# Output gates computed with tokens on partitions and 512 moving columns, split into 16-bit halves and reloaded by transposing transfers

## The chip, the cores and the metric

The kernel runs on one core of one Trainium2 chip. Inside the core, TensorE (PE) multiplies a stationary 128x128 block, loaded by a weight load (PEld), with a moving block; VectorE (DVE), ScalarE (ACT) and GpSimd (POOL) work element by element; SyncE (SP) issues most transfers between the chip's memory (DRAM) and the on-chip memory (SBUF). Products land in PSUM, eight banks of 128 partitions x 512 float32. The metric is device time in microseconds (us), the median of three runs. Transfers run on 16 DMA engines, in the order in which one queue issued them.

## The reference, cut to what matters

One layer of a diffusion backbone over T = 384 tokens (128 context, 256 latent), width D = 2048. The change touches the two sigmoid gates that merge the branches of the mixing sub-layer:

```python
gates = jax.nn.sigmoid(h @ lw['w_gate'] + lw['b_gate'])
g_a, g_b = jnp.split(gates, 2, axis=-1)
merged = g_a * (o @ lw['w_br_gla']) + g_b * (f @ lw['w_br_four'])
return merged @ lw['w_out'], s_f, s_b
```

`h` is 384 x 2048, `w_gate` 2048 x 4096. `o` comes from a gated linear attention (GLA), `f` from a Fourier branch. Everything is float32.

## The kernel before

**Products.** A float32 factor is held as two float32r parts, `hi` and `lo`, and each product is three matmuls: hi·hi, hi·lo, lo·hi. The normalised input is `hT` (tiles `A_hi`, `A_lo`), channels on partitions, 16 blocks of 128 channels by 384 tokens.

**Weight stream.** Weights come as tiles of 128 x 1024 float32 (512 KB) in the order of the list `srcs`. `load` issues one transfer into one of two `raw` buffers (L195); `split` casts it on ACT to `whi` (L223) and subtracts on DVE to get `wlo` (L224). There are four `whi` and four `wlo` buffers. `grab()` takes the oldest finished tile and, in the same breath, issues the next load and the next split. Three finished tiles stand ready while one is being multiplied, so the tile cast while tile k is multiplied is tile k+3, and its load was issued one tile earlier still, into the buffer that tile k+1 left when its `wlo` was made.

**Gate stage (L838 to L846).** For each of 32 blocks of 128 gate channels, `proj` takes two weight tiles and makes 48 matmuls into one PSUM bank of the pool `psm` (three banks, tag `mm`): stationary is a 128x128 block of weights, moving are the 384 tokens of `hT`. ACT adds the bias while it evicts to `gz` (L841), SP stores `gz` to DRAM `gates_d` (L842). After each weight tile `step(sd)` advances two side jobs by one step: `gla()`, the attention, which is cut into 61 steps by its `yield`s, and `ada`, which streams modulation weights (`adaw`, L569) into multiply-adds on DVE (L574).

**Mix stage (L1053 to L1080).** `mix_order` lists units: eight `o` (projection of the attention's output gate), sixteen `b` (`four`: Fourier products, stored to `four_d`), sixteen `a` (GLA product, multiplied by its gate, added to the Fourier part `yb`, written as `A_hi`/`A_lo` for the next projection). From the first `a` on the order is mostly b, a, a. Each `b` and `a` takes one gate: `gate_of` issues the load of a gate block (L968), for an `a` also of `yb` (L972), and takes the sigmoid of the oldest loaded one on ACT (L977). Weight tiles of `b` units are first folded on DVE (`ws`, L204 and L205).

**What sets the order.** In this part PE, ACT, DVE and POOL run strictly in the order in which the program was written; SP's order is made by a scheduler from estimated times. Every engine and every queue works in order, so an instruction that waits holds up all behind it.

Of the kernel before, what the change touches and what calls it, by code (L numbers as in the profile page):

```python
# [11 lines left out]
F32 = mybir.dt.float32  # L12
F32R = mybir.dt.float32r
U32 = mybir.dt.uint32
U16 = mybir.dt.uint16
# [6 lines left out]
P = 128  # L22
D = 2048
KT = D // P
TC = 128
TL = 256
T = TC + TL
# [70 lines left out]
def tile_step(ctx: ExitStack, tc: tile.TileContext, a, o):  # L98
# [44 lines left out]
    def two(w, i):  # L143
        return [w[i, 0], w[i, 1]]
# [4 lines left out]
    for i in range(32):  # L149
        srcs += two(a["w_gate"], i)  # L150
# [39 lines left out]
    def load(raw=None):  # L190
        n, src = next(srcs, (0, None))
        if src is not None:
            if raw is None:
                raw = wp.tile([P, G], F32, tag="raw", name="raw", bufs=2)
            SP.dma_start(raw, src)  # L195
            raws.append((raw, n in folded))
# [407 lines left out]
    gates_d = dram.tile([32, P, T], F32, name="gates_d")  # L604
# [9 lines left out]
    with ExitStack() as s:  # L614
# [23 lines left out]
        def gla():  # L638
# [10 lines left out]
            for h in range(NH):  # L649
# [12 lines left out]
                yield  # L662
# [90 lines left out]
                yield  # L753
# [32 lines left out]
                for t in range(3):  # L786
# [9 lines left out]
                    yield  # L796
# [41 lines left out]
        for i in range(32):  # L838
            def gate(p, i=i):
                g = pg.tile([P, T], F32, tag="gz", name="gz", bufs=2)  # L840
                ACT.activation(g, p, AF.Identity, bias=bgate[:, i : i + 1])  # L841
                SP.dma_start(gates_d[i], g)  # L842

            proj(psm, hT, gate, sd)
# [4 lines left out]
    four_d = dram.tile([KT, P, T], F32, name="four_d")  # L849
    with ExitStack() as s:  # L850
# [111 lines left out]
        def gate_of():  # L962

            u = next(gorder, None)
            if u is not None:
                b, i = u
                g = pc.tile([P, T], F32, tag="gate", name="gate", bufs=4)
                SP.dma_start(g, gates_d[i + (16 if b == "b" else 0)])  # L968
                y = None
                if b == "a":  # L970
                    y = pc.tile([P, T], F32, tag="yb", name="yb", bufs=4)
                    SP.dma_start(y, four_d[i])  # L972
                gates[u] = g, y
                raw_gates.append(g)
            if raw_gates and (u is None or len(raw_gates) > 1):
                g = raw_gates.pop(0)
                ACT.activation(g, g, AF.Sigmoid)  # L977
# [39 lines left out]
        for b, i in mix_order:  # L1017
            if b == "o":
                if i == 1:
                    gate_of()  # L1020
# [1002 lines left out]
```

## Time and profile before

| | us |
|---|---|
| median of 3 runs (1936.19 to 1936.66) | 1936.42 |
| the profiled execution | 1936.08 |
| its span, first to last instruction | 1934.3 |
| PE busy in the span | 1918.5 |
| matmuls of the gate stage, first to last eviction | 205.6 to 500.9 |
| mix stage, b and a units in turn | 680 to 740 |

The profile page gives busy time and counts per engine; the chain of waits follows the last instruction back to what released it; the window view gives each engine's busy time in a stretch of the span; the timeline and the tables by tile or line give single instructions and their mean durations. Where a row ends in "idle before, releaser", that is how long the engine stood still and what ended it. A matmul's own duration in the records contains its pipeline; what a run of them costs is read from the length of the run.

### The profile page before, as it was taken

Reading aid. Unit: us, or ns where it says so; the run is one execution under the profiler, and the core shown is the slowest. Engines: PE = TensorE matmul, PEld = TensorE weight load, DVE = VectorE, ACT = ScalarE, POOL = GpSimd, SP = SyncE. Lnnn points to the kernel's source line nnn. Section 1 sums busy time; section 2 is a strip of 40 time slices with the busy share of each in tenths; the row PEclk is TensorE's granted clock in tenths of the full one; section 3 lists DMA queues with packets and bytes.
Section 4 is the critical chain, followed back from the end, with each engine's and each line's share of the span. In section 5 each row is a group of like instructions: output and inputs, shape, how many; then the busy total and the mean of one; then the engine's idle time right before and its main releaser. Section 6 shows DMA issues by size and latency. Waiting matters only on the chain.

```text
span 1934.3 us, 27954 instructions
## 1 busy us (share of the span) xinstructions
PE 1918.5 (99%) x10398; PEld 1702.5 (88%) x10398; DVE 1641.8 (85%) x2059; ACT 1069.3 (55%) x1523; POOL 145.2 (8%) x171
## 2 busy tenths in 40 slices
PE   8999999999999999999999999999999999999998
PEld 5779999999999999999988888888888888888886
DVE  5569888879776797977789999999999999988885
ACT  4233454554335655446556666766666666666555
POOL 0000000000000000002100111111111120211001
PEclk9999999999999999999999999999999999999999
DMA  9978676767754687654639696979788797969553
GB/s 389 371 263 269 228 257 219 241 219 259 256 190 145 204 287 246 218 185 154 231 98 280 155 284 151 262 170 244 191 243 207 212 230 192 252 136 253 158 199 128
DMA packets 246152, 429.12 MB, mean 222 GB/s; under 512 B 45308, under 2 KB 149948, under 8 KB 241664
## 3 DMA queue, kind: packets, MB, share of 16 engines
q1 hardware_dynamic: 199072, 386.70, 60.0%
q0 software_dynamic: 18432, 33.56, 11.3%
q10 hardware_dynamic: 28512, 7.08, 2.3%
q8 instruction: 81, 1.33, 0.3%
q14 instruction: 55, 0.45, 0.1%
HBM read 365.68 MB, written 54.53 MB: 217 GB/s over the span
## 4 chain that ended last, share of the span: by engine, by line
PE 97%; DMA 1%; DVE 1%; ACT 0%; issue 0%; SPq 0%; POOL 0%; DVEq 0%; POOLq 0%; ACTq 0%
PE pmm L257 36%; PE pgu L1539 31%; PE pdn L1539 10%; PE pds L1539 7%; PE pv L399 3%; PE pgm L382 1%; PE pf L998 1%; DMA slab<-in_w_ada 1%; PE px L417 1%; PE pmm L1253 1%; PE pf L999 1%; PE bk L1539 1%; PE po L647 1%; PE pr L582 0%; PE dl L647 0%; PE pp L881 0%
## 5 line engine op out<-in xcount | busy, mean ns | idle before, releaser
L257 PE MATMUL pmm<-A_hi,whi 128*128 128x384 f32 x1200 | 404.3, 337 | 0.0
L257 PE MATMUL pmm<-A_hi,wlo 128*128 128x384 f32 x1200 | 401.4, 334 | 0.0
L257 PE MATMUL pmm<-A_lo,whi 128*128 128x384 f32 x1200 | 401.3, 334 | 0.0
L1437 ACT CAST whi<-u 128x1024 fp32r<-128x1024 f32 x200 | 210.1, 1053 | 173.1 <-PE pds L1539 42.6
L223 ACT CAST whi<-raw 128x1024 fp32r<-128x1024 f32 x181 | 189.8, 1051 | 171.3 <-DMA raw<-in_w_gate 62.2
L1448 DVE TENSOR_TENSOR wlo<-u,whi 128x1024 fp32r<-128x1024 f32 x200 | 243.7, 1220 | 34.1 <-ACT whi L1437 32.5
L224 DVE TENSOR_TENSOR wlo<-raw,whi 128x1024 fp32r<-128x1024 f32 x179 | 217.9, 1220 | 52.5 <-ACT whi L223 49.7
L1539 PE MATMUL pgu<-whi,A_hi 128*128 128x512 f32 x640 | 249.9, 390 | 0.0
L1539 PE MATMUL pgu<-whi,A_lo 128*128 128x512 f32 x640 | 249.2, 389 | 0.0
L257 PEld LDWEIGHTS pmm<-A_hi,whi 128*128 128x128 f32 x1200 | 225.3, 188 | 2.9 <-issue 1.8
L257 PEld LDWEIGHTS pmm<-A_lo,whi 128*128 128x128 f32 x1200 | 225.4, 188 | 0.2
L257 PEld LDWEIGHTS pmm<-A_hi,wlo 128*128 128x128 f32 x1200 | 225.3, 188 | 0.0
L574 DVE SCALAR_TENSOR_TENSOR adacc<-adaw,cond,adacc 128x1024 f32<-128x1024 f32 x180 | 222.7, 1278 | 2.8 <-DMA adaw<-in_w_ada 2.5
L1437 ACT CAST whi<-raw 128x1024 fp32r<-128x1024 f32 x157 | 165.0, 1053 | 87.2 <-PE pgu L1539 27.9
L1448 DVE TENSOR_TENSOR wlo<-raw,whi 128x1024 fp32r<-128x1024 f32 x157 | 191.1, 1218 | 12.6 <-ACT whi L1437 12.2
L1539 PE MATMUL pgu<-wlo,A_hi 128*128 128x512 f32 x640 | 185.8, 389 | 0.0
L1539 PEld LDWEIGHTS pgu<-whi,A_hi 128*128 128x128 f32 x640 | 120.1, 188 | 25.9 <-issue 0.8
L1539 PEld LDWEIGHTS pgu<-wlo,A_hi 128*128 128x128 f32 x640 | 120.1, 188 | 25.1
L1539 PEld LDWEIGHTS pgu<-whi,A_lo 128*128 128x128 f32 x640 | 120.1, 188 | 24.7
L1539 PE MATMUL pgu<-whi,S 128*128 128x512 f32 x400 | 116.6, 389 | 0.0
L1672 POOL DMA_DIRECT2D sums_d<-spare x64 | 58.5, 950 | 625.3 <-ACT spare L1668 618.9
L1539 PE MATMUL pdn<-whi,hid_hi 128*128 128x512 f32 x264 | 102.8, 389 | 0.0
(410 smaller groups left out, 3302.3 us busy)
## 6 DMA issues: line engine op xcount, KB each, us to landing
adaw<-in_w_ada SPq DMA_DIRECT2D x96, 512.0 KB, 4.2
raw<-in_w_d SPq DMA_DIRECT2D x70, 512.0 KB, 5.2
slab<-in_w_ada SPq DMA_DIRECT2D x32, 1024.0 KB
raw<-in_w_gate SPq DMA_DIRECT2D x64, 512.0 KB, 4.5
raw<-in_w_g SPq DMA_DIRECT2D x48, 512.0 KB, 3.7
raw<-in_w_u SPq DMA_DIRECT2D x48, 512.0 KB, 5.2
raw<-in_w_in SPq DMA_DIRECT2D x44, 512.0 KB, 4.3
u<-in_w_u SPq DMA_DIRECT2D x40, 512.0 KB, 7.1
```

What stands on the lines that cost most here:

```text
L223: ACT.copy(hi, raw)
L224: sub = lambda: eng.tensor_sub(lo, raw, hi.bitcast(F32))
L257: PE.matmul(dst, w[wi][:, k * n + n0 : k * n + n0 + P], x[xi][:, k0 + k, :], start=first and k == 0 and j == 0, stop=last and k == kts - 1 ...
L382: PE.matmul(pgv[q : q + 32, :], spad[:, k, :], slab[k // (KT // 2)][:, k % (KT // 2), :], start=k < 4, stop=k >= KT - 4,)
L399: PE.matmul(pv[2 * t + g], hT[x_][:, kb, t * P : (t + 1) * P], w_[:, g * 512 : (g + 1) * 512], start=kb == 0 and j == 0, stop=kb == KT - 1 ...
L417: PE.matmul(px, w_[:, u * P : (u + 1) * P], hT[x_][:, kb, :], start=j == 0, stop=j == 2)
L574: DVE.scalar_tensor_tensor(acc[:, c, :], w, cond[:, k, c : c + 1], acc[:, c, :], op0=ALU.mult, op1=ALU.add,)
L647: PE.matmul(dst, w[wi], x[xi], start=first and j == 0, stop=last and j == 2)
L1437: ACT.copy(hi, src)
L1448: DVE.tensor_sub(lo, src, hi.bitcast(F32))
L1539: PE.matmul(dst, stat[x_][m], mov(w[w_], m), start=first and w_ == m == x_ == 0, stop=last and w_ == m == 1, skip_group_check=any(more),)
L1672: POOL.dma_start(sums_d[k], u, accum_op=ALU.add)
```

## The change

`w_gate` is read in 64 tiles that hold four blocks of 128 gate channels and two blocks of 128 input channels, so that each partition's row is four pieces of 1 KB. For each of eight groups `q` of 512 gate channels, three PSUM banks `pgt` (128 tokens x 512 channels each, all three banks of `psm`) are filled by eight weight tiles (`m`), 18 matmuls each: stationary is a block of `hT` (128 channels x 128 tokens), moving are 512 weight columns. At m = 7, after each token block's last matmul, ACT copies the bank to `gz`, copies that as 16-bit halves, sorted, to `gpl`, and SP stores `gpl` to one of eight DRAM tensors. In the mix stage each gate block is read back by a transposing transfer (channels on partitions again), ACT puts the halves together, and the bias is now added in the sigmoid. The attention's side job has twelve `yield`s fewer (49 steps) and is not advanced at m = 6 and 7, where only `ada` is. `yb` is loaded at another place, the gate buffers are counted anew.

```diff
-    for i in range(32):
-        srcs += two(a["w_gate"], i)
+    for q in range(8):
+        for m in range(8):
+            src = a["w_gate"][4 * q : 4 * q + 4, m // 4, :, 256 * (m % 4) : 256 * (m % 4) + 256]
+            srcs.append(src.rearrange("n p x -> p n x"))
...
-    gates_d = dram.tile([32, P, T], F32, name="gates_d")
+    gates_d = [dram.tile([T, 2 * 512], U16, name=f"gates_d{n}") for n in range(8)]
...
                     SP.dma_start(s0[d], a["s0"][d, h])
-                yield
...
                     DVE.tensor_add(v, v, am[hf(c)])
-                yield
...
-                    yield
+                    if t:
+                        yield
...
-        for i in range(32):
-            def gate(p, i=i):
-                g = pg.tile([P, T], F32, tag="gz", name="gz", bufs=2)
-                ACT.activation(g, p, AF.Identity, bias=bgate[:, i : i + 1])
-                SP.dma_start(gates_d[i], g)
-
-            proj(psm, hT, gate, sd)
+        for q in range(8):
+            pt = [psm.tile([P, 512], F32, tag="mm", name="pgt") for _ in range(3)]
+            for m in range(8):
+                w = [x.rearrange("p (n k c) -> p n k c", n=4, k=2) for x in grab()]
+                for t in range(3):
+                    ts = slice(t * P, (t + 1) * P)
+                    for k in range(2):
+                        for j, (wi, xi) in enumerate(((0, 0), (0, 1), (1, 0))):
+                            PE.matmul(
+                                pt[t], hT[xi][:, 2 * m + k, ts], w[wi][:, :, k, :],
+                                start=m == k == j == 0, stop=m == 7 and k == 1 and j == 2,
+                            )
+                    if m == 7:
+                        g = pg.tile([P, 512], F32, tag="gz", name="gz")
+                        ACT.copy(g, pt[t])
+                        pl = pg.tile([P, 2 * 512], U16, tag="gpl", name="gpl", bufs=2)
+                        ACT.copy(
+                            pl.rearrange("p (n h c) -> p n h c", n=4, h=2),
+                            g.bitcast(U16).rearrange("p (n c h) -> p n h c", n=4, h=2),
+                        )
+                        SP.dma_start(gates_d[q][ts, :], pl)
+                step(ada if m in (6,7,) else sd)
...
-        def gate_of():
+        def gate_load():
 
             u = next(gorder, None)
             if u is not None:
                 b, i = u
-                g = pc.tile([P, T], F32, tag="gate", name="gate", bufs=4)
-                SP.dma_start(g, gates_d[i + (16 if b == "b" else 0)])
...
+                n = i + (16 if b == "b" else 0)
+                pl = pc.tile([P, 2 * T], U16, tag="gpl", name="gpl", bufs=4)
+                SP.dma_start(
+                    pl.rearrange("p (h t) -> p h t", h=2), gates_d[n // 4][:, 256 * (n % 4) : 256 * (n % 4) + 256],
+                    transpose=True,
+                )
+                raw_gates.append((u, pl))
...
+        def gate_of():
+
+            if raw_gates:
+                u, pl = raw_gates.pop(0)
+                b, i = u
+                n = i + (16 if b == "b" else 0)
+                g = pc.tile([P, T], F32, tag="gate", name="gate", bufs=3)
+                y = ys.pop(u, None)
+                y_load()
+                ACT.copy(
+                    g.bitcast(U16).rearrange("p (x h) -> p h x", h=2), pl.rearrange("p (h x) -> p h x", h=2),
+                )
+                ACT.activation(g, g, AF.Sigmoid, bias=bgate[:, n : n + 1])
                 gates[u] = g, y
...
+            gate_load()
```

Three places show how the instructions stand. ACT's queue in the gate stage, before: the casts of weight tiles (`whi<-raw`) with an eviction (`gz`) after every second one.

```order
L223 CAST whi<-raw 128x1024
L841 ACTIVATE gz<-pmm,bgate 128x384
L223 CAST whi<-raw 128x1024 x2
L841 ACTIVATE gz<-pmm,bgate 128x384
L702 ACT_TABLE_LOAD
```

The same queue in the changed kernel at the end of a group q; `pgt` are the three banks.

```order
L225 CAST whi<-raw 128x1024 x2
L853 COPY gz<-pgt 128x512
L855 COPY gpl<-gz 128x1024
L853 COPY gz<-pgt 128x512
L855 COPY gpl<-gz 128x1024
L853 COPY gz<-pgt 128x512
L855 COPY gpl<-gz 128x1024
L225 CAST whi<-raw 128x1024 x2
```

The evictions have moved together: six copies stand between two casts, and all of them behind the cast that the last tile's `grab` wrote.

ACT's queue in the mix stage, one group b, a, a, before (`fd` evicts the Fourier product, `A_hi` is the merged result's first part).

```order
L1002 COPY fd<-pf 128x194 x2
L223 CAST whi<-ws 128x1024
L977 ACTIVATE gate<-gate 128x384
L223 CAST whi<-raw 128x1024
L283 CAST A_hi<-yb 128x384
L977 ACTIVATE gate<-gate 128x384
```

The same stretch in the changed kernel.

```order
L1039 COPY fd<-pf 128x194 x2
L225 CAST whi<-ws 128x1024
L1009 COPY gate<-gpl 128x2x384
L1012 ACTIVATE gate<-gate,bgate 128x384
L225 CAST whi<-raw 128x1024
L285 CAST A_hi<-yb 128x384
L1009 COPY gate<-gpl 128x2x384
L1012 ACTIVATE gate<-gate,bgate 128x384
```

Each sigmoid has a copy ahead of it, which waits for a transposing transfer; the next cast of a weight tile stands behind both.

SP's queue over one such group, before.

```order
L1012 DMA four_d<-y 128x384
L968 DMA gate<-gates_d 128x384
L195 DMA raw<-in_w_br_four 128x1024
L972 DMA yb<-four_d 128x384
L968 DMA gate<-gates_d 128x384
L195 DMA raw<-in_w_br_gla 128x1024
L968 DMA gate<-gates_d 128x384
L195 DMA raw<-in_w_br_gla 128x1024
L972 DMA yb<-four_d 128x384
```

The same group in the changed kernel.

```order
L1049 DMA four_d_4629<-y 128x384
L985 DMA_TRANSPOSE gpl<-gates_d_1372 128x2x384
L998 DMA yb<-four_d_4624 128x384
L197 DMA raw<-in_w_br_four 128x1024
L985 DMA_TRANSPOSE gpl<-gates_d_1367 128x2x384
L197 DMA raw<-in_w_br_gla 128x1024 x2
L998 DMA yb<-four_d_4625 128x384
L985 DMA_TRANSPOSE gpl<-gates_d_1367 128x2x384
```

Three transposing transfers stand where three plain gate loads stood, and both loads of GLA weights now follow one of them directly.

More of the change, by code (lines that the diff above doesn't have):

```diff
@@ L837, in tile_step @@
         rate[0] = 1.0
[L838 to L844 removed]
+        for q in range(8):
[20 more added lines that the diff above has]
+                step(ada if m in (6,7,) else sd)
         for _ in gl:
             pass
[L849 removed]
+    four_d = [dram.tile([P, T], F32, name=f"four_d{n}") for n in range(KT)]
     with ExitStack() as s:
@@ L1018, in tile_step @@
             if b == "o":
[L1019 to L1020 removed]
+                if i < 2:
+                    gate_load()
+                    if i == 0:
+                        gate_load()
                 proj(psm, hT, lambda p: gcol(p, i), sd)
```

16 lines of the change are left out of this document (7 added, 9 removed).

## The prediction

> **What bounds the kernel now.** I read the page first, then the chain of waits, then windows, then single queues. The page, busy time and chain by engine:
>
> ```profile
> span 1934.3 us, 27954 instructions
> PE 1918.5 (99%) x10398; PEld 1702.5 (88%) x10398; DVE 1641.8 (85%) x2059; ACT 1069.3 (55%) x1523; POOL 145.2 (8%) x171
> PE 97%; DMA 1%; DVE 1%; ACT 0%; issue 0%; SPq 0%; POOL 0%; DVEq 0%; POOLq 0%; ACTq 0%
> ```
>
> PE works through 99% of the span and is 97% of the chain. So the time falls only where PE does its matmuls in less time, and rises only where PE is made to wait. The windows (PE, PEld, DVE, ACT, POOL, clock, DMA share, GB/s) show the two stages that the change touches, and ten-microsecond pieces at the place where PE is not full:
>
> ```profile
> 201.00:505.00 304.00, 304.00 (x1974) 299.46 (x1973) 258.81 (x329) 146.76 (x248) 1.87 (x6) 1.00 0.72 236
> 680.00:740.00 60.00, 59.28 (x359) 58.67 (x358) 53.95 (x103) 33.69 (x61) 0.00 (x0) 1.00 0.86 279
> 680.00:690.00 10.00, 9.46 (x58) 9.17 (x57) 7.46 (x18) 4.45 (x10) 0.00 (x0) 1.00 0.88 293
> 690.00:700.00 10.00, 9.81 (x60) 9.49 (x59) 9.00 (x17) 5.11 (x11) 0.00 (x0) 1.00 0.86 268
> ```
>
> In the gate stage (first row) PE never stops; DVE has 45 us of 304 free, ACT half. In the mix stage PE loses 0.54 and 0.19 us where a and b units begin to alternate, and DVE is busy 54 of 60 us: those who feed PE are at their limit there.
>
> **Term 1, the matmuls.** Pieces of the chain in order of time (start, length, what) give what a matmul costs in a run: 384 moving columns under L257, 512 under L1539, whose form (activations stationary, a strided half of a weight tile moving) is the one that the gate stage gets.
>
> ```profile
> 737.83 116.53 PE pmm L257 x672
> 1058.69 23.12 PE pgu L1539 x102
> 281.87 8.32 PE pmm L257 x48
> 454.42 4.20 PE pmm L257 x24
> ```
>
> 116.53/672 = 173.4 ns and 23.12/102 = 226.7 ns. The columns are the same in number; 32 x 48 = 1536 matmuls become 8 x 8 x 18 = 1152. 1536 x 173.4 = 266.4 us, 1152 x 226.7 = 261.1 us: **-5.2 us**, all of it on PE, which sets the end. The difference of the two lengths says why: 128 more columns cost 53.3 ns, so 384 cost 159.9 and some 13.5 ns belong to each matmul whatever its width. The gain would be nothing at 266.4/1152 = 231 ns, so 4.5 ns a matmul decide it.
>
> The Trainium skill speaks against this term: "TensorE: Matmul & The Clock Gate", section "Wait — 56ns, not 53.3ns?", puts a warm matmul at its columns over 2.4 GHz plus about 2.5 ns. By that the 384 matmuls fewer would be worth an estimated 1.0 us. The rows above disagree (13.5 ns, at a granted clock of 1.00), and I go by them.
>
> **Term 2, the three banks in the gate stage.** Before, three banks rotated and an eviction had the time of two blocks, 16.6 us (2 x 8.32). Now each group fills all three, and the next group's first matmul into a bank waits for the copy out of it. What stands ahead of these copies on ACT is the cast of a weight tile. The rows for the old eviction, for that cast (cast of tile k+3 while PE has tile k), and for what ACT waited for in this stage (total, times, longest):
>
> ```profile
> L841 ACT ACTIVATE gz<-pmm,bgate 128x384 f32<-128x384 f32 x32 | 18.6, 581 | 43.4 <-PE pmm L257 40.7 <-issue 2.6
> 282.03 1.04 ACT L223 CAST whi<-raw 128x1024 fp32r<-128x1024 f32 x1
> 459.05 1.05 ACT L223 CAST whi<-raw 128x1024 fp32r<-128x1024 f32 x1
> ACT whi L223 <- DMA raw<-in_w_gate: 57.1, 27, 6.9
> ```
>
> The copies' durations, from the same shapes later in the program (a bank of 512 columns to SBUF; 16-bit halves sorted; halves put together; the sigmoid):
>
> ```profile
> L1668 ACT COPY dw<-pds 128x512 f32<-128x512 f32 x45 | 24.3, 581 | 0.0
> L1613 ACT COPY ep<-ep 128x1024 uint16<-128x1024 uint16 x18 | 18.7, 1041 | 0.0
> L1622 ACT COPY ep<-ep 128x1024 uint16<-128x1024 uint16 x18 | 24.4, 1356 | 0.0
> L977 ACT ACTIVATE gate<-gate 128x384 f32<-128x384 f32 x32 | 16.8, 523 | 0.1
> ```
>
> A weight tile is now 18 x 226.7 = 4.08 us, 1.36 us for each token block. Count from PE's start of the tile m = 7. If the cast ends at e, the third bank is out at e + 3 x 0.58 + 2 x 1.04 = e + 3.8 us; PE wants it at 4.08 + 2 x 1.36 = 6.8. So PE waits e - 3.0 us at a group's end, nothing below. In the trace e lies between 1.2 us (tile from 281.87, cast ended 283.07) and 5.7 (tile from 454.42, cast ended 460.10), because the cast waits for its raw tile (57.1 us in 27 waits), whose buffer DVE frees late where the attention loads it. Bounds for eight ends: 0 and 8 x 2.7 = 21.6 us. Half of the ends fall behind attention steps that leave DVE free, and at m = 6 and 7 no attention step adds work, so I take nothing for four ends and the middle, e = 3.45, 0.45 us each, for four: **+1.8 us**.
>
> The rest of this stage I cost at nothing, with its cover. ACT gains 24 x (0.58 + 1.04) - 18.6 = 20.3 us in a stage in which it is idle for 157. The second `gpl` buffer makes the third sort wait for the first store, and behind it the next cast; stores land in 3.7 us, and three finished tiles (12.2 us) cover that once per 33 us. Without the cover each end would cost up to 4 us. The Fourier constants (L857) queue on SP behind the last store, as now; the raw loads behind them have the same three tiles. The twelve attention steps fewer move the same work. The rows for store, gate reload and the program's own transposing transfers, each with its time to landing, and the loads in 4 KB rows (gate weights now) and in shorter pieces:
>
> ```profile
> L842 SPq DMA_DIRECT2D gates_d<-gz x32: 326/327/425, 206.2 to 501.7; - x32
> DMA to landing us min/median/max: 2.5/3.7/5.3
> L968 SPq DMA_DIRECT2D gate<-gates_d x32: 319/424/795, 522.6 to 747.9; - x32
> DMA to landing us min/median/max: 2.4/3.9/5.8
> L1616 ACTq DMA_TRANSPOSE ep<-ep x18: 1249/1376/2142, 1050.5 to 1787.8; - x18
> DMA to landing us min/median/max: 5.3/8.9/11.7
> q1 hardware_dynamic: 199072, 386.70, 60.0%
> q10 hardware_dynamic: 28512, 7.08, 2.3%
> raw<-in_w_gate SPq DMA_DIRECT2D x64, 512.0 KB, 4.5
> raw<-in_w_g SPq DMA_DIRECT2D x48, 512.0 KB, 3.7
> raw<-in_w_u SPq DMA_DIRECT2D x48, 512.0 KB, 5.2
> ```
>
> Tiles in pieces land in 3.7 to 5.2 us, on both sides of the present 4.5: no change taken.
>
> **Term 3, the mix stage.** ACT puts each gate's halves together: 768/1024 x 1.356 = 1.02 us, 32 times. It stands ahead of the next cast. What follows shows whether that reaches PE (waits of PE in 600 to 765; ACT, then DVE, in one group b, a, a; the group's period):
>
> ```profile
> PE pmm L257 <- DVE gate L1033: 0.5, 1, 0.5
> PE pf L999 <- DVE wlo L224: 0.2, 1, 0.2
> 699.93 1.05 ACT L223 CAST whi<-ws 128x1024 fp32r<-128x1024 f32 x1 [2.81 <-DVE ws L205]
> 700.88 0.52 ACT L977 ACTIVATE gate<-gate 128x384 f32<-128x384 f32 x1
> 701.31 1.04 ACT L223 CAST whi<-raw 128x1024 fp32r<-128x1024 f32 x1
> 695.89 1.22 DVE L224 TENSOR_TENSOR wlo<-raw,whi 128x1024 fp32r<-128x1024 f32 x1 [0.90 <-ACT whi L223]
> 702.82 1.22 DVE L224 TENSOR_TENSOR wlo<-raw,whi 128x1024 fp32r<-128x1024 f32 x1
> 716.33 8.36 PE pmm L257 x48
> 727.08 8.36 PE pmm L257 x48
> ```
>
> A group lasts 10.75 us (716.33 to 727.08). The cast at 701.31 would end at 703.4 instead of 702.35; DVE wants it at 702.82, so DVE is 0.55 us late, once per group. The group's other casts had waited for DVE (2.81 us) or a raw tile, and hide the copy. Six groups: 3.3 us, out of the 6.05 us that DVE is idle in the window. Only where PE already waits, in the first two groups, does it come through: 1.1 us. The transfers add to it. Per MB a transposing one held the engines (2.3/7.08)/(60.0/386.70) = 2.1 times as long as the others. The window's seventeen gate blocks are 3.3 MB of 16.7, 0.17 of its 0.86 share; at 2.1 times, the engines are at their limit (0.86 + 0.17 x 1.1 = 1.05), and the raw loads behind them land later, as SP is also held about 1.0 us (6/8 of 1.376) instead of 0.42 for each. Bounds: 0, and 6 x 1.02 = 6 us; I take 0.8 us beside the 1.1, since DVE's idle 6 us absorb most: **+1.9 us**.
>
> On this the Trainium skill ("Advanced Engine Details and Errata", section "X-Bar Transpose (TRN2)") says that transposing transfers are as fast as regular ones. The two queue rows disagree (2.1 times). By the page the 0.8 us would go and the sum would be 0.8 us less.
>
> **Sum.** Span 1934.3, profiled execution 1936.08: 1936.1 - 5.2 + 1.8 + 1.9 = 1934.6 us. The median stands 0.3 us above the profiled execution, so the forecast is **1934.9 us**.
>
> **Rivals.**
> - *Nothing is given back* (25%): copies and transfers lie in idle time. For it: ACT half idle, every gate loaded three units ahead. Against it: the two stretches in which PE waits already. 1936.1 - 5.2 + 0.3 = 1931.2 us.
> - *The banks hold PE at every group's end* (17%): slower than before. For it: 57.1 us of waits for raw tiles ahead of these copies, and no spare bank. At e = 4.6, between the middle and the longest, 8 x 1.6 = 12.8 instead of 1.8: 1945.9 us. It decides from e = 3.4 on, at every end (8 x 0.43 us, with 1.9 in the mix stage, uses up the 5.2). Against it: PE waits only 0.7 us in all, and e was 1.2 at the easy tiles.
> - *Transposing transfers land too late* (14%): a gate is loaded three units ahead, one group, 10.75 us. Below that landing time it is hidden; above, ACT waits in every group. At 11.7, the longest seen, 6 x 0.95 = 5.7 us on top of term 2 and the 1.1: 1936.1 - 5.2 + 1.8 + 1.1 + 5.7 + 0.3 = 1939.8 us. Against it: the plain reload lands in 3.9 here, and the 8.9 belongs to a stage with much larger loads.
> - *The spacing is not saved* (6%): the fixed part per matmul is smaller here than under L1539's rows. At 1.0 us saved, 1939.1 us.
>
> **How the numbers follow.** Forecast 38%, own range 1932.5 to 1937.5. A measurement tells about 0.2% (3.9 us) from no change: below 1932.5 is faster, above 1940.3 slower. Faster: the first rival's 25 and 5 from the forecast's lower edge, 0.30. Slower: 17 from the banks, 6 from late transfers that land beyond 11.7, 2 from the forecast's upper edge, 0.25. Same: 0.45. The range goes from 1930.5 (the first rival, with attention steps that break up the matmuls less often) to 1943, which holds the late transfers and the lower part of the bank rival; some 15% lie outside.
>
> **What would show it.** Runs of `pgt` matmuls at 226 to 228 ns each show term 1. PE waits for ACT `gz` of 1 to 4 us in sum show term 2; over 8 us, the bank rival. In the mix stage PE busy of 57 to 59 in the sixty microseconds of b and a units, with ACT not waiting for the transposing transfers, shows term 3; ACT waits for `gpl` show the third rival. It is wrong if PE waits for `wlo` in the gate stage, or if the matmuls there take 230 ns or more.

## The result, and the profile after

The changed kernel takes 1960.47 us, the median of four runs (1958.69 to 1963.19), against 1936.31 us for the kernel before on the same chip: a ratio of 1.0127, 95% interval 1.0112 to 1.0142. It is slower by 24 us, where 1.5 us faster was forecast. The profiled execution took 1959.22 us. Its page, busy time and chain by engine:

```profile
span 1957.4 us, 27180 instructions
PE 1925.7 (98%) x10014; PEld 1655.7 (85%) x10014; DVE 1642.1 (84%) x2059; ACT 1125.6 (58%) x1571; POOL 145.3 (7%) x171
PE 79%; DVE 7%; DMA 6%; ACT 5%; issue 2%; SPq 0%; POOL 0%; ACTq 0%; DVEq 0%; POOLq 0%
```

PE has 384 matmuls fewer and is nevertheless busy 7 us longer, and its share of the chain falls from 97% to 79%: the chain now runs through the making of weight tiles (ACT, DVE, DMA) as well. Where the time went shows when each kernel reaches the same place in the program. The numbers are starts and ends of the named PE instructions in the two traces, in us:

| stretch | before | after | difference |
|---|---|---|---|
| up to the first gate matmul | 196.7 | 197.1 | +0.4 |
| gate stage, first matmul to the last one's end | 304.0 | 319.9 | +15.9 |
| from there to the first `px` (Fourier branch) | 20.8 | 20.7 | -0.1 |
| first `px` to the first `pst` after the mix stage (called mix stretch below) | 371.6 | 377.7 | +6.1 |
| from there to the last matmul's end | 1035.0 | 1036.4 | +1.4 |

Two thirds of the loss lie in the gate stage. Its windows (time, then busy time of PE, PEld, DVE, ACT, POOL, then granted clock, which is TensorE's clock as a share of its full speed, DMA share, GB/s): the whole stage, then five-microsecond pieces around its two longest stops.

```profile
197.10:517.00 319.90, 307.94 (x1590) 251.57 (x1590) 258.26 (x325) 166.32 (x262) 1.87 (x6) 0.98 0.70 222
317.00:322.00 5.00, 2.38 (x11) 1.63 (x9) 0.00 (x0) 1.15 (x2) 0.00 (x0) 1.00 0.54 187
322.00:327.00 5.00, 4.31 (x14) 3.49 (x15) 3.20 (x10) 4.28 (x9) 0.00 (x0) 0.71 0.32 97
442.00:447.00 5.00, 1.52 (x7) 0.94 (x5) 1.47 (x4) 3.83 (x5) 0.00 (x0) 1.00 0.35 106
447.00:452.00 5.00, 4.48 (x14) 3.81 (x15) 5.00 (x6) 4.26 (x6) 0.00 (x0) 0.50 0.10 17
452.00:457.00 5.00, 5.00 (x23) 4.18 (x23) 4.61 (x7) 0.47 (x2) 0.00 (x0) 0.82 0.67 206
```

Before, PE did not stop in this stage; now it stands 12 us. Each long stop has a second price: the pieces behind it run at a granted clock of 0.71, 0.50 and 0.82, so PE is busy and does less. Taken as the missing share of the clock, that is 5 x (0.29 + 0.50 + 0.18) = 4.9 us. DVE does nothing at all from 317 to 322, and behind the second stop (447 to 452) the loads fall to 17 GB/s: the weight stream paused as well.

What waited in the stage (waiting engine and tile, what it waited for; us in total, times, longest): DVE and ACT, then PE.

```profile
DVE wlo L226 <- ACT whi L225: 41.3, 19, 8.8
ACT gpl L855 <- DMA gates_d<-gpl: 13.2, 7, 3.9
PE bT L693 <- ACT lah L285: 4.2, 2, 3.5
PE ptm L593 <- ACT adacc L589: 3.3, 1, 3.3
PE pgt L847 <- ACT gz L853: 1.9, 2, 1.2
```

DVE's wait for `whi` was 16.1 us before:

```profile
DVE wlo L224 <- ACT whi L223: 16.1, 18, 2.9
```

PE never waits for `whi` or `wlo` in this stage: no gate matmul stood for want of a weight tile. ACT stands 13.2 us before the third sort of a group until the group's first store has landed. PE's waits for the banks (`gz`) are 1.9 us, as forecast (1.8); its two long waits are for operands of the side jobs that ACT makes: `lah`, read by the attention's matmul into `bT`, and `adacc`, read by the modulation job's matmul into `ptm`. The timeline of ACT at a group's end (start, length, line, operation, in brackets the idle time before it and what ended it) shows what they have to do with the store:

```profile
435.00 1.05 ACT L855 COPY gpl<-gz 128x1024 uint16<-128x1024 uint16 x1
436.08 0.59 ACT L853 COPY gz<-pgt 128x512 f32<-128x512 f32 x1
439.18 1.05 ACT L855 COPY gpl<-gz 128x1024 uint16<-128x1024 uint16 x1 [2.51 <-DMA gates_d<-gpl]
440.13 1.04 ACT L225 CAST whi<-raw 128x1024 fp32r<-128x1024 f32 x1
441.08 0.86 ACT L676 ACTIVATE la<-z 128x512 f32<-128x512 f32 x2
...
446.12 0.83 ACT L285 CAST lah<-la 128x768 fp32r<-128x768 f32 x1 [1.14 <-DVE la L680]
```

The store was issued at 434.38. Behind the sort that waited for it stand the cast of the next weight tile and the attention's chain up to `lah`, which ends at 446.95. PE's last gate matmul in front of the attention's `bT` ran out at 443.5, and it stood 3.48 us until 447.00, though gate matmuls stood behind `bT` in its queue whose `wlo` DVE had finished by 442.44. The stop at 319 is the same with `adacc`; the third sort, what ACT does behind it, and the matmul that waits for that:

```profile
321.32 1.04 ACT L855 COPY gpl<-gz 128x1024 uint16<-128x1024 uint16 x1 [3.85 <-DMA gates_d<-gpl]
322.27 0.37 ACT L589 COPY adacc<-pr 128x256 f32<-128x256 f32 x1
322.69 0.44 PE L593 MATMUL ptm<-ident,adacc 128*128 128x128 f32 x2 [3.32 <-ACT adacc L589]
```

The mix stage loses in another way. PE's waits in it, then one turn of ACT, SP and DVE through a group b, a, a (PE's own group is 10.75 us long):

```profile
PE pf L1036 <- DVE wlo L226: 5.2, 5, 1.4
717.19 1.05 ACT L225 CAST whi<-ws 128x1024 fp32r<-128x1024 f32 x1 [3.12 <-DVE ws L207]
718.15 1.07 ACT L1009 COPY gate<-gpl 128x768 uint16<-128x768 uint16 x1
719.25 0.62 ACT L1012 ACTIVATE gate<-gate,bgate 128x384 f32<-128x384 f32 x1
719.77 1.03 ACT L225 CAST whi<-raw 128x1024 fp32r<-128x1024 f32 x1
720.70 0.51 ACT L285 CAST A_hi<-yb 128x384 fp32r<-128x384 f32 x1
721.12 1.07 ACT L1009 COPY gate<-gpl 128x768 uint16<-128x768 uint16 x1
722.21 1.21 SPq L985 DMA_TRANSPOSE gpl<-gates_d  x1
723.54 0.50 SPq L998 DMA_DIRECT2D yb<-four_d  x1
724.15 0.37 SPq L197 DMA_DIRECT2D raw<-in_w_br_four  x1
728.26 0.69 DVE L206 TENSOR_TENSOR ws<-raw 128x512 f32<-128x512 f32 x1 [1.71 <-DMA raw<-in_w_br_four]
729.59 1.05 ACT L225 CAST whi<-ws 128x1024 fp32r<-128x1024 f32 x1 [3.35 <-DVE ws L207]
```

Follow it down: cast, gate copy, sigmoid, cast, `A_hi`, the second gate copy; 0.02 us after that copy's end SP issues the next transposing reload, which had waited for it; behind it in SP's queue stand `yb` and the Fourier weights' load, whose tile lands at 728.2, is folded, and can be cast at 729.59. That is a closed loop of 729.59 - 717.19 = 12.4 us in which nothing waits for PE, and it is longer than PE's 10.75. It holds for the other groups too: from 690 to 765, 16 of 18 reloads start 0.03 us after the end of a gate copy, and the casts of folded tiles are 12.3 us apart on average (705.03 to 754.28). SP's wait for ACT ahead of the reloads, which the profile puts down to the instruction behind the copy, the sigmoid:

```profile
SPq L985 <- ACT gate L1012: 19.7, 11, 3.3
```

### The profile page after: what moved, and what is told of

Same layout as the page of the kernel before. It is cut to its first block, busy times and chain, and to the rows that moved or that the text cites. A ratio compares the mean times of both kernels' runs of the same rounds, so it can differ in the third digit from the quotient of the medians.

```text
span 1957.4 us, 27180 instructions
## 1 busy us (share of the span) xinstructions
PE 1925.7 (98%) x10014; PEld 1655.7 (85%) x10014; DVE 1642.1 (84%) x2059; ACT 1125.6 (58%) x1571; POOL 145.3 (7%) x171
## 4 chain that ended last, share of the span: by engine, by line
PE 79%; DVE 7%; DMA 6%; ACT 5%; issue 2%; SPq 0%; POOL 0%; ACTq 0%; DVEq 0%; POOLq 0%
PE pgu L1578 31%; PE pmm L259 16%; PE pdn L1578 10%; PE pds L1578 7%; PE pgt L847 6%; PE pv L401 3%; DVE adacc L576 2%; DMA raw<-in_w_gate 2%; DVE wlo L226 2%; ACT whi L225 2%; PE pgm L384 1%; DMA raw<-in_w_br_four 1%; DMA slab<-in_w_ada 1%; PE px L419 1%; DMA gates_d<-gpl 1%
## 5 line engine op out<-in xcount | busy, mean ns | idle before, releaser
L1476 ACT CAST whi<-u 128x1024 fp32r<-128x1024 f32 x200 | 210.2, 1053 | 168.3 <-PE pgu L1578 38.7
L259 PE MATMUL pmm<-A_hi,whi 128*128 128x384 f32 x688 | 231.4, 336 | 0.0
L259 PE MATMUL pmm<-A_lo,whi 128*128 128x384 f32 x688 | 230.1, 334 | 0.0
L259 PE MATMUL pmm<-A_hi,wlo 128*128 128x384 f32 x688 | 230.0, 334 | 0.0
L847 PE MATMUL pgt<-whi,A_hi 128*128 128x512 f32 x384 | 153.3, 399 | 2.1 <-ACT gz L853 1.9
L847 PE MATMUL pgt<-wlo,A_hi 128*128 128x512 f32 x384 | 151.2, 394 | 0.0
L847 PE MATMUL pgt<-whi,A_lo 128*128 128x512 f32 x384 | 151.1, 394 | 0.0
L259 PEld LDWEIGHTS pmm<-A_hi,whi 128*128 128x128 f32 x688 | 129.2, 188 | 1.1 <-issue 1.0
L259 PEld LDWEIGHTS pmm<-A_lo,whi 128*128 128x128 f32 x688 | 129.2, 188 | 0.5 <-DVE A_lo L286 0.2
L259 PEld LDWEIGHTS pmm<-A_hi,wlo 128*128 128x128 f32 x688 | 129.1, 188 | 0.0
```

The source lines that it names most:

```text
L259: PE.matmul(dst, w[wi][:, k * n + n0 : k * n + n0 + P], x[xi][:, k0 + k, :], start=first and k == 0 and j == 0, stop=last and k == kts - 1 ...
L847: PE.matmul(pt[t], hT[xi][:, 2 * m + k, ts], w[wi][:, :, k, :], start=m == k == j == 0, stop=m == 7 and k == 1 and j == 2,)
L1476: ACT.copy(hi, src)
```

## The experiments

Each time is the median of four runs (the last but one: ten). Ratios are against the kernel before, run beside it, with 95% intervals. Gate stage and mix stretch are measured as in the table above, in one profiled execution of each, and such an execution can lie off the median: 1953.4 us for the third sort buffer, 1961.2 for the halves on POOL, 1953.9 for the side bank (some 7 of its 8 us too many lie behind the mix stretch). In the eight runs that have the change's mix stage unaltered the mix stretch is 377.7 to 381.0 us, so differences of 3 us in it are not told from none.

| run | time, us | ratio | gate stage | PE idle in it | mix stretch |
|---|---|---|---|---|---|
| change | 1960.5 | 1.0112 to 1.0142 | 319.9 | 12.0 | 377.7 |
| third sort buffer | 1949.8 | 1.0056 to 1.0086 | 310.8 | 5.9 | 381.0 |
| six reload buffers | 1962.0 | 1.0115 to 1.0145 | 320.2 | 12.2 | 381.4 |
| steps as before | 1964.7 | 1.0134 to 1.0165 | 324.6 | 15.5 | 379.4 |
| sort on POOL | 1956.0 | 1.0079 to 1.0113 | 316.2 | 8.2 | 378.9 |
| no copy of the halves | 1957.8 | 1.0093 to 1.0127 | 318.4 | 10.8 | 376.2 |
| plain reload | 1956.2 | 1.0086 to 1.0116 | 320.9 | 11.8 | 375.8 |
| copies ahead of the cast | 1959.7 | 1.0104 to 1.0134 | 320.6 | 10.6 | 378.0 |
| halves on POOL | 1956.4 | 1.0093 to 1.0123 | 309.7 | 4.2 | 386.3 |
| third buffer, steps as before | 1951.2 | 1.0052 to 1.0086 | 314.9 | 7.1 | 378.6 |
| sort out of the bank | 1948.8 | 1.0051 to 1.0082 | 308.6 | 6.9 | 380.1 |
| evictions only | 1940.6 | 1.0013 to 1.0031 | 309.3 | 5.9 | 371.5 |
| side bank | 1945.7 | 1.0029 to 1.0063 | 306.3 | 3.9 | 379.6 |

**A third sort buffer.** It takes the place of a tile that the gate stage no longer uses.

```diff
-pl = pg.tile([P, 2 * 512], U16, tag="gpl", name="gpl", bufs=2)
+pl = pg.tile([P, 2 * 512], U16, tag="gpl" if t < 2 else "a2part", name="gpl", bufs=2 if t < 2 else 1)
```

> A third buffer for the sorted halves (in the space of a tile that the gate stage no longer uses), so that the third sort of a group does not wait for the group's first store. Theory 'store': ACT stands 13.2 us in that wait (7 times), and the attention's matmuls, whose operands ACT makes behind it, hold PE (3.5 us at 443, 3.3 us at 319, and the lower clock after these stops, 0.50 and 0.71 in the next five microseconds, some 5 us more). Then the gate stage falls from 320 us to 308 to 312 us and the time to 1948 to 1952 us. Rival 'density' (the attention's steps now sit in 48 tiles out of 64): the wait only covers a lack that would come anyway; the time falls by less than 3 us, to above 1957 us.

Measured: 1949.84 us, 10.6 us less, inside the store theory's 1948 to 1952. ACT's wait for the store no longer appears, and PE's waits in the stage are:

```profile
PE pgt L847 <- ACT gz L853: 2.5, 2, 2.0
PE bT L693 <- ACT lah L285: 1.7, 2, 1.0
PE bT L693 <- DVE lal L286: 1.3, 2, 0.7
```

The wait of 3.5 us for `lah` is down to 1.0 and that for `adacc` is gone. The intervals are apart (at most 1.0086 against at least 1.0112). So the store's wait on ACT was the largest single loss of the change. Some 7 us over the kernel before remain in the stage.

**The attention's steps as before**, alone and together with the third buffer: the twelve yields put back, and one step after every tile.

```diff
+                yield
...
-                step(ada if m in (6,7,) else sd)
+                step(sd)
```

> The attention's twelve yields are put back and its side job is advanced at every weight tile, as before the change; the group's six copies and the two sort buffers stay. Theory 'store': the waits at the group's ends stay and may hit more attention steps; the time stays within 4 us of the change's 1960. Rival 'density': the gate stage falls by 8 to 12 us, to 1948 to 1952 us.

> Three sort buffers together with the attention's steps as before (61 steps, one after every weight tile). Alone the steps made the change 4 us slower. If that loss came from the store's wait hitting more steps, then without the wait the steps cost nothing: the time is within 2 us of 1949.8. If attention steps behind the group's end are a cost of their own (the tiles m = 6 and 7 then have no room for the copies), the loss stays: 1952 to 1956. If density is a cost after all, 1944 to 1947.

Measured: alone 1964.71 us, 4.2 above the change and so just past the 4 us that the store theory allowed; with the third buffer 1951.23, 1.4 above the run with that buffer. In both pairs the intervals overlap. The density rival falls, since it wanted 8 to 12 us less. That more steps cost only where the sort waits for a store isn't shown: the profiled gate stage is longer by 4.7 us with the wait and by 4.1 without it.

**The sort on POOL**, with three sort buffers.

```diff
-                        ACT.copy(
+                        POOL.tensor_copy(
                             pl.rearrange("p (n h c) -> p n h c", n=4, h=2),
```

> As the run with three sort buffers, but POOL sorts the halves, so that ACT keeps only the three plain copies of a group (1.05 us x 24 taken off ACT). If only the store's wait counted, it is within 1.5 us of the run with three sort buffers. Theory 'copies' (ACT's own 5 us at each group's end delay the casts and the attention): 3 to 6 us below that run. Rival: POOL's sort is slow or slows DVE by sharing its way to the memory, and the run is above it.

Measured: 1955.95 us, 6.1 above the run with ACT's sort, as the rival had it. The group of the sort (durations min/median/max, then first and last start), a wait of ACT, and the stage's window:

```profile
L855 POOL COPY gpl<-gz x24: 1041/1298/2730, 231.8 to 515.2; 128x1024 uint16<-128x1024 uint16 x24
ACT gz L853 <- POOL gpl L855: 25.6, 16, 2.8
196.70:512.90 316.20, 308.01 (x1591) 251.43 (x1590) 268.86 (x325) 142.94 (x239) 33.18 (x29) 0.98 0.71 225
```

Two costs came with it. The single `gz` buffer makes ACT wait for POOL, 25.6 us, so ACT's queue is as blocked as before; and DVE is busy 268.9 us instead of 258.4 with the same instructions. The run doesn't tell what ACT's own copy time is worth, nor which of the two costs weighs more.

**The copies ahead of the cast**, with three sort buffers: at m = 7 the next load and cast are written behind the six copies.

```diff
-                w = [x.rearrange("p (n k c) -> p n k c", n=4, k=2) for x in grab()]
+                w = [x.rearrange("p (n k c) -> p n k c", n=4, k=2) for x in (take() if m == 7 else grab())]
...
+                if m == 7:
+                    push()
```

> The run with three sort buffers, and at the last weight tile of a group the next load and cast are written behind the six copies instead of ahead of them, so that the evictions no longer stand behind a cast that waits for its raw tile (PE waited 2.5 us for gz there, 2.0 us at one end). Theory 'banks': PE's waits for gz go, and the time falls by 2 to 4 us below that run's 1949.8. Rival: the cast is now up to 5 us later at each end, DVE starves for it and the attention waits more; the time is the same or up to 8 us above it.

Measured: 1959.72 us, 9.9 above the run with the buffer alone: the rival, and more. PE's waits for `gz` are gone, and the attention pays:

```profile
PE bT L693 <- ACT lah L285: 7.0, 3, 2.8
```

ACT waits 25.2 us for PE ahead of its copies in this run, with the cast behind them. So in this run too, where PE itself blocks ACT at the group's end, the loss comes back through the attention.

**Sorting out of the bank.** The plain copy falls away, and there are three sort buffers.

```diff
-                        g = pg.tile([P, 512], F32, tag="gz", name="gz")
-                        ACT.copy(g, pt[t])
-                        pl = pg.tile([P, 2 * 512], U16, tag="gpl", name="gpl", bufs=2)
+                        pl = pg.tile([P, 2 * 512], U16, tag="gpl", name="gpl", bufs=3)
...
-                            g.bitcast(U16).rearrange("p (n c h) -> p n h c", n=4, h=2),
+                            pt[t].bitcast(U16).rearrange("p (n c h) -> p n h c", n=4, h=2),
```

> The halves are sorted straight out of the PSUM bank into three sort buffers: the plain copy (24 x 0.58 us) is gone, a bank comes free after one copy, and no store is waited for. Theory 'ACT's queue at the group's end' (what stands ahead of casts and attention there sets the rest of the loss): 5.0 us of copies become 3.2 us if a sort from the bank takes the same 1.05 us, the gate stage falls from 310.7 to 304 to 308 us and the time to 1943 to 1947. Rival: a bank is read slower in 16-bit halves (1.5 us or more each), and the time is 1949 or above.

Measured: 1948.79 us; the intervals of this run and of the one with the third buffer lie on each other, so the gain in the total is not told from none. The gate stage is 308.6 us. Both figures lie just past the theory's upper bounds (1947 and 308). The rival's slow bank is not there, and the banks now hold PE:

```profile
L853 ACT COPY gpl<-pgt x24: 1000/1012/1030, 232.3 to 505.5; 128x1024 uint16<-128x1024 uint16 x24
PE pgt L847 <- ACT gpl L853: 4.9, 3, 2.0
```

**A side bank**, on top of that: the first of the three banks comes from the attention's five.

```diff
-        pt = [psm.tile([P, 512], F32, tag="mm", name="pgt") for _ in range(3)]
+        pt = [psm.tile([P, 512], F32, tag="mm", name="pgt") if n else pss.tile([P, 512], F32, tag="side", name="pgt") for n in range(3)]
```

> The run that sorts straight out of the banks, with the first of a group's three banks taken from the attention's five (so the next group's first matmuls need not wait for this group's last evictions; the attention works with four). Theory 'banks': PE's waits for the evictions (4.9 us in that run, with three restarts) fall below 1.5 us, the gate stage from 308.6 to 303 to 305 us and the time from 1948.8 to 1943 to 1946. Rival: the attention, with a bank less, waits for its own banks as long, and the time stays at 1948 or above.

Measured: 1945.72 us, gate stage 306.3. The bank waits are gone:

```profile
PE pgt L847 <- ACT gpl L853: 0.2, 1, 0.2
```

So the banks are real, but the second thing, not the first: 4.9 us of waits once the store's wait is away. The time is inside the theory's 1943 to 1946; the gate stage misses its 303 to 305, where one wait of 2.3 us for `lah` now stands. The interval reaches that of the run above, so the 3 us in the total are not told from none; the wait rows and the 2.3 us in the gate stage, one execution of each, are what speaks for the gain. It is the fastest version found that still computes the layer in full precision, and 9.8 us slower than the kernel before.

**Six reload buffers** in the mix stage.

```diff
-pl = pc.tile([P, 2 * T], U16, tag="gpl", name="gpl", bufs=4)
+k = n_gpl[0] % 6
...
+if k < 4:
+    pl = pc.tile([P, 2 * T], U16, tag="gpl", name="gpl", bufs=4)
+else:
+    pl = pc.tile([P, 4 * T], U16, tag="fs", name="gpl", bufs=2)[:, 0 : 2 * T]
```

> Six buffers instead of four for the transposing reload in the mix stage, so that SP does not stand before a reload until ACT has put the previous halves together; everything else as in the change. Theory 'loop': copy on ACT, transposing issue on SP, the Fourier weights' load behind it, its landing, folding, cast and again copy make a loop of 12.2 us per group where PE needs 10.75; with it open, PE's waits for wlo there fall from 5.2 us to below 1 us and the time falls by 4 to 6 us, to 1953 to 1957 us. Rival 'engines': the transposing transfers load the DMA engines and the raw tiles land late anyway; the change is below 1.5 us.

Measured: 1961.99 us, no difference that can be told. The edit didn't open the loop: SP's order is made by a scheduler, and in it most reloads still wait for a copy (from 690 to 765, 11 of 17 start 0.03 us after a gate copy's end). That the scheduler placed them where it expected a buffer to come free is the likely reason, but not shown (SP's and PE's waits in 690 to 765 and from 500 on):

```profile
SPq L990 <- ACT gate L1017: 20.9, 12, 3.0
PE pf L1041 <- DVE wlo L226: 6.4, 5, 1.5
```

It tells the two theories apart in neither direction.

**Without the copy of the halves, and with a plain reload**, one each.

```diff
-                ACT.copy(
-                    g.bitcast(U16).rearrange("p (x h) -> p h x", h=2), pl.rearrange("p (h x) -> p h x", h=2),
-                )
-                ACT.activation(g, g, AF.Sigmoid, bias=bgate[:, n : n + 1])
+                ACT.activation(g, pl[:, T : 2 * T].bitcast(mybir.dt.bfloat16), AF.Sigmoid, bias=bgate[:, n : n + 1])
```

> The change with ACT's copy that puts the halves together left out: the sigmoid reads the upper 16 bits of each gate alone (so the gates are rounded); the transposing reloads stay. With six reload buffers SP still issued each reload just behind ACT's copy, since SP's order puts a load where its buffer is expected to come free; so the loop (ACT copies, reload issue, Fourier weights' load behind it, folding, cast) was not opened there. Theory 'loop': two copies of 1.07 us fewer in it bring it from 12.2 to some 10.1 us, below PE's 10.75; PE's waits for wlo in the mix stage fall from 5.2 us to below 1 us and the time by 4 to 6 us, to 1954 to 1956. Rival 'transfers' (the transposing transfers alone make the raw tiles late): the waits stay above 3 us and the time above 1957.

```diff
-                SP.dma_start(
-                    pl.rearrange("p (h t) -> p h t", h=2), gates_d[n // 4][:, 256 * (n % 4) : 256 * (n % 4) + 256],
-                    transpose=True,
-                )
+                SP.dma_start(pl, gates_d[n // 4][0:P, 0 : 2 * T])
...
-                    g.bitcast(U16).rearrange("p (x h) -> p h x", h=2), pl.rearrange("p (h x) -> p h x", h=2),
+                    g.bitcast(U16).rearrange("p (n c h) -> p n h c", n=3, h=2), pl.rearrange("p (n h c) -> p n h c", n=3, h=2),
```

> The change with a plain reload of as many bytes instead of the transposing one (so the gates go to wrong tokens and channels); the copy of the halves on ACT stays. Theory 'loop': a plain issue holds SP 0.4 instead of 1.21 us, so the loop goes from 12.2 to 11.4 us, still above 10.75: PE's waits for wlo in the mix stage fall to 2 to 4 us and the time by 1 to 3 us. Rival 'transfers': the waits fall below 1 us and the time by 4 to 6 us.

The copy's pattern is changed as well; it lasts as long as before (1072 instead of 1070 ns). Measured: 1957.75 and 1956.21 us, so 2.7 and 4.3 less than the change, with intervals that reach the change's; PE's waits for `wlo` there (the first of the two rows is the run without the copy):

```profile
PE pf L1033 <- DVE wlo L226: 2.8, 4, 1.4
```

```profile
PE pf L1033 <- DVE wlo L226: 2.5, 4, 0.8
```

Neither expectation holds in full. Without the copy the waits should have gone and halved. With the plain reload they halved, as the loop had it, but the time fell by more than the 3 us allowed. The loop as it was written down, with one way through it, was too simple: when one link is shorter, the reload still waits on SP for ACT (for the sigmoid, in the run without the copy). The casts of folded tiles were 11.3 us apart without the copy (the loop had been reckoned at 10.1) and 11.9 with the plain reload (reckoned 11.4).

**Evictions only**: both of these left out together, and the sort too (three `gz` buffers, stored as they are; the sigmoid takes 16-bit numbers from the wrong places).

```diff
-                        pl = pg.tile([P, 2 * 512], U16, tag="gpl", name="gpl", bufs=2)
...
-                        SP.dma_start(gates_d[q][ts, :], pl)
+                        SP.dma_start(gates_d[q][ts, :], g.bitcast(U16))
```

> The change with the sort left out in the gate stage (three buffers for the plain copy, which is stored as it is) and, in the mix stage, with a plain reload and no copy of the halves, the sigmoid reading 16-bit numbers of the wrong places (so the gates are wrong). What is left is the matmuls' new shape, the piecewise weight loads, three plain evictions a group and the store. Theory: the gate stage is 302 to 306 us (sorts and store wait were its loss), the mix stage like before's (PE's waits there below 1 us), and the time 1932 to 1938. Rival: the three banks and DVE's and the loads' pace cost by themselves; the gate stage stays above 308 us and the time above 1940.

Measured: 1940.57 us. PE's waits in the mix stage, and a window of it:

```profile
PE pmm L259 <- DVE gate L1061: 0.3, 1, 0.3
PE pf L1025 <- DVE wlo L226: 0.2, 1, 0.2
680.00:755.00 75.00, 74.48 (x449) 73.75 (x448) 65.66 (x127) 42.89 (x72) 0.00 (x0) 1.00 0.87 281
```

The mix stretch is 371.5 us, the 371.6 of the kernel before. So copy and transposing reload together are the whole of the loss there, which was 6.1 to 9.8 us in the runs that have both on ACT and SP. The gate stage, though, is the rival's, and so is the time: 309.3 us with no sort at all, about what the third buffer alone gives. The sorts' own 25 us on ACT are thus not what holds it; PE still waits for the banks there:

```profile
PE pgt L847 <- ACT gz L853: 4.0, 4, 1.8
```

**The halves on POOL**, with three sort buffers: `POOL.tensor_copy` in place of ACT's copy in the mix stage.

> The run with three sort buffers, and POOL instead of ACT puts the halves together in the mix stage. Theory 'loop': ACT's part of the loop is shorter by the two copies, as without the copy, and the time falls by 4 to 6 us below that run's 1949.8, to 1944 to 1946. Rival: POOL's copies slow DVE (in the run with POOL's sort, DVE's busy time in the gate stage rose from 258 to 269 us with the same work) where DVE has only 6 us of 60 free; the time stays at 1949 or rises to 1953.

Measured: 1956.44 us, 6.6 above the run with the buffer alone, and a mix stretch of 386.3: the rival's direction, and more than its 1953. DVE's subtraction from 590 to 780, in that run and then in the one with the copies on ACT (count, busy us, mean ns, idle before):

```profile
L226 DVE TENSOR_TENSOR wlo<-raw,whi 128x1024 fp32r<-128x1024 f32 x29 | 46.9, 1619 | 10.0 <-ACT whi L225 10.0
```

```profile
L226 DVE TENSOR_TENSOR wlo<-raw,whi 128x1024 fp32r<-128x1024 f32 x32 | 38.9, 1223 | 17.3 <-ACT whi L225 17.3
```

## Why the prediction was wrong

**Term 1 (-5.2 us) had the right price for a matmul, but not for the stage.** Undisturbed runs of 18 `pgt` matmuls start 4.08 us apart, 226.7 ns each, as taken. But all neighbouring `pgt` matmuls together, PE's idle time taken out, are 233.8 ns apart on average (before: 174.8 for `pmm`), over the 230 ns that the prediction named as its refutation. Split by the starts of single matmuls, in us (gate matmuls: mean distance of neighbours, for those with attention work between them the undisturbed one):

| | gate matmuls | attention between them | PE idle | sum |
|---|---|---|---|---|
| before | 268.3 | 35.2 | 0.0 | 303.5 |
| change | 268.9 | 38.7 | 12.0 | 319.5 |
| third sort buffer | 267.4 | 37.1 | 5.9 | 310.4 |
| sort out of the bank | 264.2 | 37.1 | 6.9 | 308.2 |
| evictions only | 266.0 | 37.0 | 5.9 | 308.9 |
| side bank | 265.1 | 36.9 | 3.9 | 305.9 |

The only one of these new kernels without a stretch of low clock in this stage, the sort out of the bank, gains 4.1 us on the gate matmuls; the change loses 0.6. The term needed a PE that never stops, and the stops took it away: of the 7.8 us between 268.9 and the ideal 261.1, some 18 matmuls at 427 ns behind the two long ones are 18 x 0.20 = 3.6 us. Much of the rest are single matmuls, behind short stops and behind attention work, that took some 335 ns instead of 227.

**Term 2 (+1.8 us) was right for the wait it priced**: PE's waits for `gz` are 1.9 us. That the sum fits so well is partly luck: it was reckoned as four waits of 0.45 us and came as two, of 1.2 and 0.7. The step that failed is the paragraph behind it, "the rest of this stage I cost at nothing", and in it this sentence: the third sort waits for the first store, "and behind it the next cast; stores land in 3.7 us, and three finished tiles (12.2 us) cover that". The tiles did cover the late cast: PE never waited for a weight tile. They don't cover what else stands in ACT's queue behind the sort: `lah` and `adacc`, for which a matmul stands in PE's queue ahead of gate matmuls that could have run. With the clock behind the stops this was worth 10.6 us of the time (the run with the third buffer). The prediction had named the length of such a wait, "up to 4 us" an end (the longest was 3.9), and put it at nothing. A smaller miss beside it: a store is 256 KB now instead of 192 and landed in 4.5 us, not 3.7. The twelve steps fewer were not the cause: putting them back made neither kernel faster.

**Term 3 (+1.9 us) was 6.1 to 9.8 us.** The step that failed: the copy comes through only in the first two groups, "since DVE's idle 6 us absorb most". The order of SP's queue was read, but the reload was not followed as a wait: it stands before the Fourier weights' load until ACT's copy has freed a buffer, so copy and issue (1.07 and 1.21 us) lie in a loop with the load, the folding and the cast, and not in idle time of single engines. Six groups at up to 1.6 us of lateness (12.3 against 10.75) are its price, of which PE's waits for `wlo` show 5.2. With copy and transposing reload both left out the whole loss is gone. With one left out, the mix stretch is 1.5 and 1.9 us shorter, which one execution of each can't tell from none, so how the loss divides between them stays open.

**The rivals.** The banks held PE 1.9 us, not 12.8: false for the change, though they come next (4.9 us) where the store's wait is away. Transposing transfers did not land too late: ACT never waited for one in the mix stage. Where they stand in the way is SP's queue, 1.21 us an issue, with the loads behind them. The spacing's saving was lost, but to the clock and the stops: undisturbed, the matmuls stood at 226.7 ns, so the fixed part was not smaller.

**The sum.** Forecast -5.2 + 1.8 + 1.9; measured +15.9 in the gate stage, +6.1 in the mix stretch and 1.1 in small differences elsewhere, together the 23.1 us by which the span grew. The range (1930.5 to 1943) missed, since its bounds were made of the waits that had been named, and the largest one had been put at nothing.

What stays open: with no store's wait and hardly a bank wait (the side bank), the gate stage is still 306.3 us against 304.0 before and an ideal of 261.1 + 35.2 = 296.3. The table divides this into 4.0 us of slower gate matmuls, 1.7 of longer attention stretches and 3.9 of idle time. A stretch of low clock (0.66 from 292.5 to 297.5) behind PE's wait for the attention is in it; no run took the parts apart. Nor was it tested whether the loads in pieces have a share: they land in 4.7 us instead of 4.5, and ACT's waits for raw gate tiles, 57.1 us before, are 71.1 in the change and 79.5 in the run with the side bank, though PE waited for no weight tile. The price of ACT's sort time alone was not isolated on POOL.

## What to carry to other kernels

When an instruction that may wait is put into an engine's queue, list everything behind it on that queue and ask for each who waits for it: a cover counted in finished tiles holds only for those who use the tiles, and not for other work that another in-order engine has interleaved. A buffer that comes free through the same engine whose next work needs the load behind it makes a loop; compare the loop's length with the bound engine's period, not each part with idle time. Here a gain of some nanoseconds per matmul was there only while the matmuls ran without a break, so price stops together with the slow clock behind them.

## What the hardware showed beside that

- **The clock behind a stop.** After stops of 3.3 and 3.5 us, matmuls of 512 columns came 426 to 427 ns apart instead of 227, for 3 to 4 us, at a granted clock down to 0.50. The Trainium skill ("TensorE: Matmul & The Clock Gate", section "What's actually happening") says that PE falls to half its clock after an idle window of about 3.4 us, and in the section "Wait — 56ns, not 53.3ns?" it has 426.7 ns for 512 columns at that clock, which is what the trace shows. But a stop of 1.96 us was enough in the run with three sort buffers (up to 467.56), where the five microseconds behind it show 0.66, while behind a stop of the same length in the run that sorts out of the bank (up to 466.96) the clock stayed at 1.00. So the length of one stop doesn't decide it alone; what else does isn't shown:

```profile
467.50:472.50 5.00, 4.94 (x15) 3.91 (x16) 4.03 (x4) 4.84 (x7) 0.00 (x0) 0.66 0.90 288
```

- **POOL's copies slow DVE.** In the stretch in which POOL copied between SBUF tiles (590 to 780), DVE's subtraction took 1619 ns on average instead of 1223. The Trainium skill ("SBUF — State Buffer", section "SBUF: two separate sides") tells of a pair of ports that DVE's instructions with two SBUF inputs share with POOL, whole instruction by whole instruction; the rows fit that, though they don't show the ports.
- **A bank can be sorted as 16-bit halves as fast as SBUF**: 1012 ns out of PSUM, 1047 ns out of SBUF, for the same 128 x 1024 halves on ACT.
